# Four transposes per token tile and layer in a two-layer decoder trunk, taken from TensorE to VectorE blocks and DMAs

## The chip, the cores and the metric

The kernel runs on one core of one Trainium2 chip. The metric is the device time of one execution in microseconds (us). The time before is 1190.25 us, the median of three runs (1189.96 to 1190.47). All arithmetic is in float32; products are made from a rounded upper part and a remainder of each operand (type float32r), three matmuls for each product.

## The reference, cut to what matters

The program computes two layers of a decoder trunk over 256 tokens of width 1024. Each layer is a feed-forward part, a mixer and a second feed-forward part, each between two RMS norms. Only the mixer is touched, and in it two things: the short convolution, and the gated sum of the three branches on its way into the output projection.

```python
u, bg, cg, q, kv, nsa_g, q_mem, merge_g = jnp.split(h @ w_in, points, axis=-1)
y_conv = bg * short_conv(cg * u, conv_w)          # conv3 along the tokens, 512 channels
...
g_conv, g_nsa, g_mem = jnp.split(jax.nn.sigmoid(merge_g), 3, axis=-1)
merged = g_conv * (y_conv @ w_br_conv) + g_nsa * (y_nsa @ w_br_nsa) + g_mem * (y_mem @ w_br_mem)
return merged @ w_out
```

## The kernel before, in words

The 256 tokens are two tiles of 128, t = 0 and t = 1. Each tile has a stream of its own through both layers (`stream`, generator functions), and the program is written by a loop that advances one stream by one step at a time. A step is mostly one weight unit: a tile of 128x1024 weights is loaded by SyncE into `raw`, ScalarE rounds it into `whi` (L333), VectorE makes the remainder `wlo` (L334), and TensorE multiplies. Every unit is used by both streams, stream 0 being up to `LEAD` = 3 steps ahead. Splits of units are written `AHEAD` = 4 steps before their use. `later(n, fn)` puts a piece of work n steps on, counted over both streams. Attention, compression and the memory branch run as background tasks between the steps. The order in which each engine finally sees its instructions comes from the framework's scheduler, which works with modelled durations (two of its constants are set at the head of the file); SyncE alone keeps the order written.

A matmul of this kernel has tokens in columns of its left operand, so activations have to be turned from tokens-in-partitions to channels-in-partitions. There are two ways in the kernel before:

- `transpose4` (L441): TensorE multiplies four blocks of 128x128 with an identity into one bank of PSUM, and ScalarE and VectorE read the bank.
- `turn` (L451 to L457): the source is written in an order of columns called lanes (`lanes_out` of the target, `lanes_in` of what is read: every fourth column first), VectorE turns its 32x32 blocks (`nc.vector.transpose`, in the trace STREAM_TRANSPOSE), one step later (`AWAY` = 1) GpSimd issues four DMAs from `blocks` to `moved`, which carry the blocks to their partitions, and after `wait` steps the given function reads `moved`.

In the mixer (`mixer`, L1382 on), stream by stream:

- u is scaled into `us`, then `conv_part` multiplies it with the columns of c into `v`, and `CONV` = 7 steps later transposes `v` with `transpose4`; from the bank come `vT` (with two carried tokens in front) and `cT`, the sum over the three taps.
- `conv_out` scales the columns of the gate into `bs`, `BS` = 4 steps later transposes it, multiplies `cT` with it and splits the product into `yconv`, which the branch product reads after two more column blocks of gates (16 steps over both streams).
- For each branch in `ORDER` and each half n of the 1024 output columns, `gth` times the branch product is summed into `merged0` and `merged1` (L1435 to L1438). After the last branch `transpose_half` transposes half 0 `HALF` = 5 steps later, half 1 at `SECOND` = 2 steps into the output projection, and `evac_split` (L432, L433) splits the bank into `mThi` and `mTlo`.
- `output` multiplies with `w_mix_out` in eight steps k; steps 0 to 3 read half 0, steps 4 to 7 half 1. The last three steps are written bank by bank (`TAIL`).

## Time and profile before

| | |
|---|---|
| median of three runs | 1190.25 us |
| the profiled execution | 1190.01 us |
| its span on the core | 1188.3 us, so 1.7 us lie around it |
| TensorE matmul busy | 1177.2 us, 5777 instructions |
| VectorE busy | 891.7 us |
| ScalarE busy | 755.9 us |
| GpSimd busy | 177.2 us |
| moved by DMA | 260.64 MB |
| granted TensorE clock | 0.999 of full speed |

In the rows of the profile PE is TensorE's matmul queue, PEld its weight load, DVE VectorE, ACT ScalarE, POOL GpSimd, SP SyncE; L441 is line 441 of the kernel before. A group gives its busy time in us and the mean of one instruction in ns, then the idle time of its engine just before it and what ended that. Matmuls overlap, so a matmul's own duration is longer than the distance to the next one.

### The profile page before, as it was taken

To read this page: it belongs to the slowest core of one execution; us is meant where nothing else is said; L and a number is where in the kernel's file an instruction comes from. 1 tells how busy PE (TensorE), PEld (TensorE's weight loads), DVE (VectorE), ACT (ScalarE), POOL (GpSimd) and SP (SyncE) were. 2 spreads that over 40 slices of the span, in tenths; PEclk is the share of its full clock that TensorE was granted. 3 is DMA by queue.
4 is the path that set the end of the run, shared out by engine and by line. 5 is a ranking of instruction groups with operands and counts; after the bars stand their busy time and mean duration, and the time that the engine had idled before them with its cause. 6 is when DMAs were issued, how large, how long until landed. Compare 5 with 4: busy or idle time off the path is not lost.

```text
span 1188.3 us, 16619 instructions
## 1 busy us (share of the span) xinstructions
PE 1177.2 (99%) x5777; PEld 1032.5 (87%) x5777; DVE 891.7 (75%) x1130; ACT 755.9 (64%) x1217; POOL 177.2 (15%) x333
## 2 busy tenths in 40 slices
PE   9999999999999999999999999999999999999997
PEld 7888888888988888888888888889888888888886
DVE  6867757798998786676577677588899977767753
ACT  6655836888885565555465565469889655655541
POOL 4001301411120020011011011014012200110100
PEclk9999999999999999999999999999999999999999
DMA  7787875776678767777767678757767687587771
GB/s 258 253 256 240 276 261 154 228 240 192 194 231 216 247 185 221 222 235 230 228 184 230 215 229 270 240 141 242 232 178 229 198 231 229 178 250 213 234 223 63
DMA packets 133764, 260.64 MB, mean 219 GB/s; under 512 B 15694, under 2 KB 36848, under 8 KB 133680
## 3 DMA queue, kind: packets, MB, share of 16 engines
q1 hardware_dynamic: 124048, 235.11, 63.7%
q0 software_dynamic: 9600, 24.47, 7.6%
q8 instruction: 45, 0.74, 0.3%
q14 instruction: 39, 0.32, 0.1%
q10 hardware_dynamic: 32, 0.01, 0.0%
HBM read 235.42 MB, written 2.10 MB: 200 GB/s over the span
## 4 chain that ended last, share of the span: by engine, by line
PE 95%; ACT 2%; DVE 1%; issue 1%; DMA 0%; POOL 0%; SPq 0%; DVEq 0%; POOLq 0%; ACTq 0%
PE acc L410 35%; PE acc L396 9%; PE acc L397 9%; PE acc L398 9%; PE y L398 7%; PE y L396 7%; PE y L397 7%; PE pt L441 2%; PE br L396 2%; PE br L398 2%; PE br L397 2%; ACT whi L333 1%; PE s L1070 1%; DVE wlo L334 0%; PE om L1268 0%
## 5 line engine op out<-in xcount | busy, mean ns | idle before, releaser
L334 DVE TENSOR_TENSOR wlo<-raw,whi 128x1024 fp32r<-128x1024 f32 (+2 forms) x441 | 529.0, 1211 | 186.0 <-ACT whi L333 182.0
L333 ACT CAST whi<-raw 128x1024 fp32r<-128x1024 f32 (+2 forms) x441 | 452.6, 1040 | 255.2 <-PE acc L410 116.1
L457 POOL DMA_DIRECT2D moved<-blocks x176 | 95.8, 563 | 644.6 <-DVE blocks L451 368.9
L410 PE MATMUL acc<-wlo,hThi 128*128 128x512 f32 x640 | 191.6, 380 | 0.0
L410 PE MATMUL acc<-whi,hTlo 128*128 128x512 f32 x640 | 191.4, 380 | 0.0
L410 PE MATMUL acc<-whi,hThi 128*128 128x512 f32 x640 | 191.4, 381 | 0.0
L396 PE MATMUL acc<-whi,hThi 128*128 128x512 f32 (+1 forms) x480 | 182.8, 381 | 0.0
L397 PE MATMUL acc<-wlo,hThi 128*128 128x512 f32 (+1 forms) x480 | 179.3, 374 | 0.3 <-DVE wlo L334 0.2
L398 PE MATMUL acc<-whi,hTlo 128*128 128x512 f32 (+1 forms) x480 | 178.9, 373 | 0.0
L410 PEld LDWEIGHTS acc<-whi,hTlo 128*128 128x128 f32 x640 | 121.2, 189 | 17.3 <-DVE hTlo L513 0.4
L410 PEld LDWEIGHTS acc<-wlo,hThi 128*128 128x128 f32 x640 | 121.1, 189 | 17.0 <-DVE wlo L334 0.3
L410 PEld LDWEIGHTS acc<-whi,hThi 128*128 128x128 f32 x640 | 120.7, 189 | 16.6
L396 PE MATMUL y<-whi,turnhi 128*128 128x512 f32 x352 | 133.8, 380 | 0.0
L397 PE MATMUL y<-wlo,turnhi 128*128 128x512 f32 x352 | 133.7, 380 | 0.0
L398 PE MATMUL y<-whi,turnlo 128*128 128x512 f32 x352 | 133.7, 380 | 0.0
L398 PEld LDWEIGHTS acc<-whi,hTlo 128*128 128x128 f32 x480 | 90.9, 189 | 11.6
L397 PEld LDWEIGHTS acc<-wlo,hThi 128*128 128x128 f32 x480 | 91.1, 190 | 10.9 <-DVE wlo L334 0.9
L396 PEld LDWEIGHTS acc<-whi,hThi 128*128 128x128 f32 x480 | 91.1, 190 | 10.3
L398 PEld LDWEIGHTS y<-whi,turnlo 128*128 128x128 f32 x352 | 66.7, 189 | 9.2
L397 PEld LDWEIGHTS y<-wlo,turnhi 128*128 128x128 f32 x352 | 66.7, 189 | 9.2
L396 PEld LDWEIGHTS y<-whi,turnhi 128*128 128x128 f32 x352 | 66.7, 189 | 9.2
L475 DVE TENSOR_TENSOR turnlo<-moved,turnhi 128x1024 fp32r<-128x1024 f32 (+1 forms) x42 | 49.1, 1168 | 26.8 <-ACT turnhi L474 26.4
(307 smaller groups left out, 1449.6 us busy)
## 6 DMA issues: line engine op xcount, KB each, us to landing
raw<-in_ffn_w_in_dram SPq DMA_DIRECT2D x159, 512.0 KB, 4.7
raw<-in_w_mix_in_dram SPq DMA_DIRECT2D x96, 512.0 KB, 4.5
raw<-in_ffn_w_out_dram SPq DMA_DIRECT2D x88, 512.0 KB, 4.6
moved<-blocks POOLq DMA_DIRECT2D x144, 128.0 KB, 4.3
raw<-in_ffn_w_in_dram SPq DMA_DIRECT2D x34, 256.0 KB, 4.0
raw<-in_w_mem_kv_dram SPq DMA_DIRECT2D x16, 512.0 KB, 4.6
raw<-in_w_mix_out_dram SPq DMA_DIRECT2D x16, 512.0 KB, 4.9
raw<-in_cmp_k_w_dram SPq DMA_DIRECT2D x8, 512.0 KB, 4.6
```

The source lines that it names most:

```text
L333: pinned(nc.scalar.copy(hi[:, c0:c1], raw[:, c0:c1]))
L334: pinned(nc.vector.tensor_sub(lo[:, c0:c1], raw[:, c0:c1], f32(hi[:, c0:c1])))
L396: nc.tensor.matmul(ps, lhsT=xh, rhs=wh, start=start, stop=False, skip_group_check=skip)
L397: nc.tensor.matmul(ps, lhsT=xh, rhs=wl, start=False, stop=False, skip_group_check=skip)
L398: nc.tensor.matmul(ps, lhsT=xl, rhs=wh, start=False, stop=stop, skip_group_check=skip)
L410: pinned(nc.tensor.matmul(ps[j][:, :n], lhsT=hT[x2][:, k], rhs=moving(w, j * n, n), start=(k == 0 and i == 0), stop=(k == 7 and i == 2)))
L441: pinned(nc.tensor.transpose(pt[:, j * P:(j + 1) * P], src[:, c0 + j * P:c0 + (j + 1) * P], ident))
L457: nc.gpsimd.dma_start(moved[0][:, q * f:(q + 1) * f], blocks[q * 32:(q + 1) * 32, :n].rearrange("j (p f) -> j p f", p=4))
L475: nc.vector.tensor_sub(lv, mv, f32(hv))
L1070: nc.tensor.matmul(s3[:, i], lhsT=QT[:, g * 2 + u, i], rhs=pairs(KT[j][:, var * 2 + g], 0, 256), start=(i == 0 and j == 0), stop=(i == 1 a ...
```

## The change

`v` and `bs` are written in lanes and go through `turn` instead of `transpose4`; the waits `CONV` and `BS` become 9 steps. The sum of a half after the last branch goes into a new tile `laned` in lanes, which goes through `turn` as well, with a wait of 11 steps for half 0 and 8 for half 1 (`MOVED`); what reads `moved` is `place`, and if it hasn't run by then, the output's step 0 (half 0) or step 4 (half 1) runs it. `cT` is now made from `vT` in SBUF, since no bank holds the turned `v`. The factors of the norm are placed so that `v` needs no scale of its own (`r[4]` is the product of two of them).

```diff
+MOVED = {0: 11, 1: 8}
-CONV, BS, CMP, ZC, QS_0, QS_1, QM, PC, YM = 7, 4, 6, 2, 2, 6, 2, 3, 1
+CONV, BS, CMP, ZC, QS_0, QS_1, QM, PC, YM = 9, 9, 6, 2, 2, 6, 2, 3, 1
...
         v = ttile("v")
-        nc.vector.scalar_tensor_tensor(v[:, :512], c_ps, r[0], u_s[:, :512], op0=OP.mult, op1=OP.mult)
+        nc.vector.tensor_tensor(lanes_out(v, 0, [[P, 4]]), lanes_in(u_s, 0, 512), lanes_in(c_ps, 0, 512), op=OP.mult)
         cT = ttile("cT")
-        def turn():
-            pt = transpose4(v, 0)
+        def shifted(mv):
...
-            nc.scalar.copy(vT[:, :, 2:130], pt.rearrange("p (c s) -> p c s", c=4))
+            nc.scalar.copy(view(vT, 2, [[130, 4], [32, 4], [1, 32]]), mv)
...
-                nc.scalar.activation(dst, pt[:, c * P:(c + 1) * P], AF.Copy, scale=w[2])
+                nc.scalar.activation(dst, vT[:, c, 2:130], AF.Copy, scale=w[2])
...
-        later(CONV, turn)
+        turn(v, 512, shifted, CONV)
...
-        nc.scalar.activation(bs[:, :512], b_ps, AF.Copy, scale=r[1])
-        def turn():
-            pt = transpose4(bs, 0)
-            nc.vector.tensor_tensor(cT[:, :512], cT[:, :512], pt, op=OP.mult)
+        nc.scalar.activation(lanes_out(bs, 0, [[P, 4]]), lanes_in(b_ps, 0, 512), AF.Copy, scale=r[0])
+        def gated(mv):
+            nc.vector.tensor_tensor(quarters(cT[:, :512], 4), quarters(cT[:, :512], 4), mv, op=OP.mult)
...
-        later(BS, turn)
+        turn(bs, 512, gated, BS)
...
-        nc.scalar.activation(u_s[:, :512], ps, AF.Copy, scale=r[0])
+        nc.scalar.activation(u_s[:, :512], ps, AF.Copy, scale=r[4])
...
+        def move_half(n, laned, wait):
+            def place(mv):
+                if placed[n]:
+                    return
+                placed[n] = True
+                sl = slice(n * 512, (n + 1) * 512)
+                hv, lv = quarters(mh[:, sl], 4), quarters(ml[:, sl], 4)
+                nc.scalar.copy(hv, mv)
+                nc.vector.tensor_sub(lv, mv, f32(hv))
+            moved = turn(laned, 512, place, wait)
+            return lambda: place(turned_view(moved[0], 512))
...
-                    nc.vector.tensor_add(dst, dst, th[:, :512])
+                    if b == ORDER[2] and n in MOVED:
+                        laned = ttile("laned")
+                        nc.vector.tensor_tensor(lanes_out(laned, 0, [[P, 4]]), lanes_in(merged[n], 0, 512),
+                                                lanes_in(th, 0, 512), op=OP.add)
+                        last_half[n] = move_half(n, laned, MOVED[n])
+                    else:
+                        nc.vector.tensor_add(dst, dst, th[:, :512])
...
         def between(k):
-            if k == SECOND:
+            if k == 0 and 0 in MOVED:
+                last_half[0]()
+            if k == 4 and 1 in MOVED:
+                last_half[1]()
```

Three places show what the scheduler makes of it. The first is VectorE's order in the first layer around the second stream's `v`: `us` and `acc` are its two factors, `pc`, `phc` and `nmm` belong to attention, `cT` is the convolution's sum. Before:

```order
L1284 SCALAR_TENSOR_TENSOR v<-acc,rs,us 128x512
L1207 TENSOR_TENSOR phc<-pt,phc 32x512
L1245 TENSOR_REDUCE nmm<-sm 128x2
L1303 SCALAR_TENSOR_TENSOR cT<-vT,convT,cT 128x128 x2
L1304 SCALAR_TENSOR_TENSOR cT<-vT,convT,cT 128x128 x2
```

Now:

```order
L1285 TENSOR_TENSOR v<-us,acc 128x512
L1246 TENSOR_REDUCE nmm<-sm 128x2
L452 STREAM_TRANSPOSE blocks<-v 128x512
L1208 TENSOR_TENSOR phc<-pt,phc 32x512
L1246 TENSOR_REDUCE nmm<-sm 128x2
L335 TENSOR_TENSOR wlo<-raw,whi 128x1024
L452 STREAM_TRANSPOSE blocks<-bs 128x512
```

The block transposes of `v` and of the first stream's `bs` stand among the splits `wlo`, and the first `cT` has moved four instructions down.

The second place is VectorE's order in the first layer from the sum of half 1 on, stream 0 first (`merged_3092` before, `merged_3086` now), then stream 1. Before:

```order
L433 TENSOR_TENSOR mTlo<-pt,mThi 128x512
L1437 SCALAR_TENSOR_TENSOR gth<-gth,br 128x512
L334 TENSOR_TENSOR wlo<-raw,whi 128x1024
L1438 TENSOR_TENSOR merged_3092<-merged_3092,gth 128x512
L334 TENSOR_TENSOR wlo<-raw,whi 128x1024 x2
L1437 SCALAR_TENSOR_TENSOR gth<-gth,br 128x512
L1438 TENSOR_TENSOR merged_3209<-merged_3209,gth 128x512
L334 TENSOR_TENSOR wlo<-raw,whi 128x1024
L433 TENSOR_TENSOR mTlo<-pt,mThi 128x512
```

Now:

```order
L1452 SCALAR_TENSOR_TENSOR gth<-gth,br 128x512
L1418 TENSOR_TENSOR mTlo<-moved,mThi 128x512
L335 TENSOR_TENSOR wlo<-raw,whi 128x1024
L1455 TENSOR_TENSOR laned<-merged_3086,gth 128x512
L452 STREAM_TRANSPOSE blocks<-laned 128x512
L335 TENSOR_TENSOR wlo<-raw,whi 128x1024 x2
L1452 SCALAR_TENSOR_TENSOR gth<-gth,br 128x512
L335 TENSOR_TENSOR wlo<-raw,whi 128x1024
L1455 TENSOR_TENSOR laned<-merged_3198,gth 128x512
L335 TENSOR_TENSOR wlo<-raw,whi 128x1024
L452 STREAM_TRANSPOSE blocks<-laned 128x512
L1418 TENSOR_TENSOR mTlo<-moved,mThi 128x512
```

Between the product `gth` and the block transpose now stand a remainder of the other stream's half 0 and one split (stream 0), or two splits (stream 1). In the second layer stream 0 has the same company, stream 1 one split.

The third place is TensorE's order in the first layer where stream 1's output comes to half 1 (its step 4; `y0_4252` and `y1_4253` before, `y0_4270` and `y1_4271` now). Before:

```order
L396 MATMUL y0_4194<-whi_4278,mThi_3093 128x512
L397 MATMUL y0_4194<-wlo_4279,mThi_3093 128x512
L398 MATMUL y0_4194<-whi_4278,mTlo_3094 128x512
L396 MATMUL y0_4252<-whi_4231,mThi_3210 128x512
L397 MATMUL y0_4252<-wlo_4232,mThi_3210 128x512
L398 MATMUL y0_4252<-whi_4231,mTlo_3211 128x512
```

Now:

```order
L397 MATMUL y1_4210<-whi_4321,mThi_3087 128x512
L398 MATMUL y1_4210<-wlo_4322,mThi_3087 128x512
L397 MATMUL y0_4270<-whi_4253,mThi_3199 128x512
L398 MATMUL y0_4270<-wlo_4254,mThi_3199 128x512
L397 MATMUL y1_4271<-whi_4253,mThi_3199 128x512
L399 MATMUL y0_4270<-whi_4253,mTlo_3200 128x512
```

Step 4 of stream 1 has gone behind stream 0's last step, and within it the matmuls that read `mThi` come before the first that reads `mTlo`. Counted in TensorE's order of the first layer, 54 matmuls now stand between the last branch matmul of half 1 and the output's step 4 in stream 0 and 59 in stream 1; in the second layer 54 and 52.

More of the change, by code (lines that the diff above doesn't have):

```diff
@@ L1401, in mixer @@
         merged = [ttile(f"merged{n}") for n in range(2)]
+        last_half = [None, None]
         mh, ml = gtile("mThi", F32R), gtile("mTlo", F32R)
@@ L1406, in transpose_half @@
             evac_split(mh[:, sl], ml[:, sl], transpose4(merged[n], 0))
+        placed = [False, False]
+        def move_half(n, laned, wait):
[9 more added lines that the diff above has]
+            return lambda: place(turned_view(moved[0], 512))
         for b in ORDER:
@@ L1437, in mixer @@
                     nc.vector.scalar_tensor_tensor(th[:, :512], th[:, :512], 1.0, pb, op0=OP.add, op1=OP.mult)
-                    nc.vector.tensor_add(dst, dst, th[:, :512])
-                if b == ORDER[2] and n == 0:
+                    if b == ORDER[2] and n in MOVED:
[5 more added lines that the diff above has]
+                        nc.vector.tensor_add(dst, dst, th[:, :512])
+                if b == ORDER[2] and n == 0 and 0 not in MOVED:
                     later(HALF, lambda: transpose_half(0))
@@ L1444, in between @@
         def between(k):
-            if k == SECOND:
+            if k == 0 and 0 in MOVED:
+                last_half[0]()
+            if k == 4 and 1 in MOVED:
+                last_half[1]()
+            if k == SECOND and 1 not in MOVED:
                 transpose_half(1)
```

## The prediction, made before the changed kernel had run

> **What bounds the kernel now.** I read the page first, then TensorE's waits, then the windows of the two mixers, and last single instructions in the timeline. From the page: the span, the engines' busy times, the chain that ended last.
>
> ```profile
> span 1188.3 us, 16619 instructions
> PE 1177.2 (99%) x5777; PEld 1032.5 (87%) x5777; DVE 891.7 (75%) x1130; ACT 755.9 (64%) x1217; POOL 177.2 (15%) x333
> PE 95%; ACT 2%; DVE 1%; issue 1%; DMA 0%; POOL 0%; SPq 0%; DVEq 0%; POOLq 0%; ACTq 0%
> ```
>
> 95% of the chain is TensorE. A busy matmul queue could still be stretched by waits, so the view of its waits is next:
>
> ```profile
> PE pt L441 <- DMA x<-in_x_dram: 1.4, 1, 1.4
> PE idle L205 <- DVE idle L200: 1.1, 1, 1.1
> PE z L1111 <- DVE wlo L334: 1.0, 2, 0.6
> PE pt L441 <- POOL kd L905: 0.4, 1, 0.4
> ```
>
> The four longest kinds of wait make 3.9 us. The kernel's time is therefore the number of matmuls times their spacing, and a matmul taken away is time gained, as long as the others come as early as before. But the mixers, where the change sits, have VectorE close behind:
>
> ```profile
> 280.00:350.00 70.00, 70.00 (x375) 62.27 (x375) 66.90 (x110) 61.19 (x135) 11.34 (x23) 1.00 0.68 207
> 350.00:400.00 50.00, 50.00 (x239) 43.59 (x238) 42.10 (x50) 30.46 (x43) 4.33 (x8) 1.00 0.81 228
> 870.00:950.00 80.00, 80.00 (x421) 70.94 (x420) 77.36 (x117) 67.56 (x148) 16.51 (x31) 1.00 0.66 195
> ```
>
> (Windows; the columns after the length are PE, PEld, DVE, ACT, POOL, then clock, DMA share and GB/s.) VectorE is free for 3.1 us of 70 around the first layer's convolution and 2.6 of 80 around the second's; 7.9 of 50 are free afterwards.
>
> **The change part by part. Removed: 64 transposes.** Groups of TensorE by tile, one group of four in the timeline, and an unbroken stretch of the chain in order of time:
>
> ```profile
> L441 PE MATMUL pt<-ident,merged 128*128 128x128 f32 x32 | 4.8, 273 | 0.0
> L441 PE MATMUL pt<-ident,bs 128*128 128x128 f32 x16 | 2.7, 273 | 0.0
> L441 PE MATMUL pt<-ident,v 128*128 128x128 f32 x16 | 2.4, 273 | 0.0
> 288.54 0.60 PE L441 MATMUL pt<-ident,v 128*128 128x128 f32 x4
> 288.89 0.46 PE L396 MATMUL acc<-whi,hThi 128*128 128x512 f32 x1
> 289.19 0.38 PE L397 MATMUL acc<-wlo,hThi 128*128 128x512 f32 x1
> 289.41 0.38 PE L398 MATMUL acc<-whi,hTlo 128*128 128x512 f32 x1
> ...
> 431.13 95.19 PE acc L410 x441
> ```
>
> 64 instructions are 16 groups of four. An undisturbed 128x512 matmul takes 95.19/441 = 0.216 us. From the start of the group to the second matmul behind it are 0.65 us; less one matmul the group costs 0.434 us (the first matmul behind it is stretched too). 16 x 0.434 = **6.9 us off TensorE**.
>
> The Trainium skill, page TensorE: Matmul & The Clock Gate, section Part 4: PE-mode transpose, has about 275 ns for a transpose in a kernel; the rows' mean of 273 ns agrees. An estimate from that page's figure is 64 x 0.275 = 17.6 us; it prices latency where the queue pays spacing, 0.109 us each here, so I don't use it.
>
> **Added on VectorE.** Rows by form, and one of ScalarE's:
>
> ```profile
> L451 DVE STREAM_TRANSPOSE blocks<-wide 128x1024 f32<-128x1024 f32 x16 | 19.8, 1239 | 0.0
> L451 DVE STREAM_TRANSPOSE blocks<-wide 128x768 f32<-128x768 f32 x8 | 7.8, 975 | 0.1
> L1284 DVE SCALAR_TENSOR_TENSOR v<-acc,rs,us 128x512 f32<-128x512 f32 x4 | 3.0, 746 | 0.0
> L1438 DVE TENSOR_TENSOR merged<-merged,gth 128x512 f32<-128x512 f32 x16 | 10.9, 684 | 0.3
> L1095 DVE TENSOR_TENSOR F<-G,smallT 128x240 f32<-128x240 f32 x8 | 4.2, 572 | 0.1
> L579 DVE TENSOR_TENSOR hTlo<-hf,hThi 128x256 fp32r<-128x256 f32 x20 | 8.1, 420 | 0.6
> L579 DVE TENSOR_TENSOR hTlo<-hf,hThi 128x512 fp32r<-128x512 f32 x10 | 6.9, 685 | 0.0
> L816 ACT COPY mp<-m 128x1024 f32<-128x1024 f32 x2 | 5.9, 2949 | 0.0
> L333 ACT CAST whi<-raw 128x1024 fp32r<-128x1024 f32 x431 | 446.4, 1049 | 255.1 <-PE acc L410 116.1 <-PE y L398 67.5 <-PE acc L398 34.4
> ```
>
> A block transpose of 512 columns is one more step of 256 down the line: 0.975 - 0.264 = 0.71 us. Four for each token tile and layer.
>
> `v` and the two `laned` now read SBUF at every fourth column. No VectorE row does just that. L1095 reads with a wider step: a packed read of 240 would take 0.403 us on the line through L579's rows (0.420 - 16 x 0.00104), it takes 0.572, so 0.70 ns more for an element. ScalarE's L816 reads every fourth column: 2.949 against 1.049 us packed, 1.86 ns more for an element. So a strided 512 on VectorE costs between 0.69 (no penalty) and 1.64 us (ScalarE's); I take 1.05 us (0.685 + 512 x 0.0007), the same engine's row. The Trainium skill, page SBUF — State Buffer, section Door 1: The DMA port swizzle, says that SBUF has lines of 16 bytes, and each access that crosses to a new one pays; a step of four floats does so every time. Rows L816 and L1095 agree, which speaks against the free end.
>
> Per tile and layer: 4 x 0.71 + (1.05 - 0.746) + 2 x (1.05 - 0.684) = 3.9 us, of which `v` and `bs` bring 1.72 (bounds 1.36 and 2.31). Where the weight splits have time this costs nothing. The cushion can be counted: splits made, and matmuls that read `wlo` (four for each split, two from each stream), up to a given time:
>
> ```profile
> 0.00:310.00 310.00, 154.82 (x458) 84.09 (x458) 139.49 (x118) 1.00 0.74 232
> 0.00:945.00 945.00, 481.90 (x1403) 260.68 (x1403) 424.77 (x355) 1.00 0.73 224
> ```
>
> At 310 us 117 splits are made (two of the 118 instructions are halves) and 458/4 = 114.5 used up. Up to three splits wait half used for the stream that is three steps behind, 1.5, so 1.0 is ahead: 12 matmuls, 2.6 us. At 945 us it is 354 - 350.75 - 1.5 = 1.75, so 4.5 us. Against this stand, for two tiles, 3.44 us more VectorE and 4 x 0.434 = 1.74 us by which TensorE comes earlier. Of VectorE's free time I take half as usable, since what ends it is mostly ScalarE's `whi`, which comes no earlier now: 1.5 and 1.3 us. First layer: 3.44 + 1.74 - 1.5 - 2.6 = **1.1 us given back**; second: 3.44 + 1.74 - 1.3 - 4.5, below nothing, so 0. Bounds: 0 (all free time used), and 4.62 + 1.74 - 2.6 = 3.8 plus 4.62 + 1.74 - 4.5 = 1.9, so 5.7. The `laned` sums and their blocks, 4 x (1.05 + 0.71 - 0.684) = 4.3 us a layer, fall behind 350 us into the 7.9 free ones; without that cover they would cost 4.3 us a layer.
>
> **The new wait: half 1 before output step 4.** TensorE, VectorE and a turn in the timeline:
>
> ```profile
> 397.40 0.38 PE L398 MATMUL br<-whi,ynsa 128*128 128x512 f32 x1
> 397.82 0.69 DVE L1437 SCALAR_TENSOR_TENSOR gth<-gth,br 128x512 f32<-128x512 f32 x1
> 398.43 1.22 DVE L334 TENSOR_TENSOR wlo<-raw,whi 128x1024 fp32r<-128x1024 f32 x1
> 360.58 1.24 DVE L451 STREAM_TRANSPOSE blocks<-p 128x1024 f32<-128x1024 f32 x1
> 369.41 1.04 ACT L474 CAST turnhi<-moved 128x1024 fp32r<-128x1024 f32 x1 [2.35 <-DMA moved<-blocks]
> 122.06 0.98 DVE L451 STREAM_TRANSPOSE blocks<-wide 128x768 f32<-128x768 f32 x1
> 129.43 0.84 ACT L474 CAST turnhi<-moved 128x768 fp32r<-128x768 f32 x1 [1.02 <-DMA moved<-blocks]
> L432 ACT CAST mThi<-pt 128x512 fp32r<-128x512 f32 x8 | 4.7, 586 | 6.9 <-PE pt L441 6.9
> L457 POOL DMA_DIRECT2D moved<-blocks x176 | 95.8, 563 | 644.6 <-DVE blocks L451 368.9 <-issue 125.0 <-PE y L398 36.7
> ```
>
> From the end of a block transpose to the reader that waited for the DMAs are 7.59 us (1024 columns) and 6.39 (768); four issues of 0.56 us are in it. For 512 I take 6.39, nearest in size. Budget of stream 0: 54 matmuls x 0.216 = 11.66 us after the last branch matmul ends its turn (397.62). Chain: 0.20 to `gth`, 0.69, the other `mTlo` 0.69, a split 1.22, `laned` 1.05, blocks 0.71, turn 6.39, `mThi` 0.59: 11.54 us, just in time; `mTlo`, 0.69 later, is due two matmuls later (12.09) and 0.14 late. Stream 1 has 59 (12.74 us) and two splits in front: 12.07. Second layer: 11.54 against 11.66, and 10.85 against 52 matmuls, 11.23. Sum about 0.3 us; with 7.59 for the turn the latenesses of `mTlo` are 1.3, 0.6, 1.3 and 1.1, together 4.3. I take **1.0 us**, nearer the smaller transfer. While ScalarE waits in `mThi`, its next `whi` casts stand behind it, and VectorE's `wlo` and later TensorE behind those; the cushion there is filling, as VectorE's 7.9 free us show. Half 0 has 78 matmuls, 16.8 us.
>
> `vT` and `gated` also wait for DMAs, but nine steps (some 1.3 us each) after the blocks against 6.39 to 7.59. On GpSimd 64 more issues are 36 us on 177 of 1188; behind its copy into `carry`, which waits for `vT`, stand `bs`'s four issues, with seven steps in hand. The 4.2 MB more are 1.6% of the bytes. These I price at nothing; if `bs` came ten steps late, `yconv` would block two branch products, 2.6 us.
>
> **Sum**, against the profiled execution of 1190.0 us (span 1188.3, 1.7 around it, 0.24 under the median of the runs): 1190.0 - 6.9 + 1.1 + 1.0 = **1185.2 us**.
>
> **The rivals.** (a) All is hidden: 1190.0 - 6.9 = 1183.1. For it: no wait for `wlo` between 280 and 400 us. Against: VectorE's 95% there. (b) VectorE becomes the bound around the convolutions, strided reads at ScalarE's price: 1190.0 - 6.9 + 5.7 + 1.0 = 1189.8, no difference. For it: L816. Against: L1095. (c) Slower: the halves come late. Place: `mThi` before output step 4. With 7.59 us for each turn and a split more (1.22) in front of each, four halves lose 4.3 + 4.9 = 9.2, and the casts blocked behind ScalarE's wait one split time (1.2) in each of two layers: 1190.0 - 6.9 + 1.1 + 11.6 = 1195.8. It decides from 1.7 us of lateness a half. For it: budgets with a tenth to spare. Against: it needs every turn at its slowest. (d) A transpose held the queue for its whole 273 ns: 1190.0 - 17.5 + 2.1 = 1174.6. Against: the starts at 288.54 and 288.89. That the change doesn't do what it says is excluded by the orders shown: no `v`, `bs` or `merged` is left on TensorE.
>
> **How the numbers follow.** Forecast 0.56, (a) 0.14, (b) 0.17, (c) 0.12, (d) 0.01. A measurement of this kernel tells about 0.2% (2.4 us) from no change. The forecast's own range, both given-back terms from 0.4 to 4.5 together, is 1183.5 to 1187.6, all faster; with (a) and (d), and little of (b), faster is 0.70; same 0.18, from (b) and the near end of (c); slower 0.12. Range 1182.8 to 1191.0: (a), the forecast and (b) whole, (c) mostly left out.
>
> **What would show it.** 5713 matmuls; TensorE's waits in the mixers about 2 us, half for `wlo` between 300 and 350 us, half for `mThi` or `mTlo`; block transposes of 512 at 0.71; `laned` and `v` at 1.05; VectorE about 907 us busy. Waits for `mThi` of over 1.7 us each, or VectorE without a gap through both mixers, would prove it wrong; so would strided sums at 1.6.

## The result and the profile after

The changed kernel takes 1201.37 us (median of four runs, 1200.30 to 1201.50), the kernel before 1190.36 (four runs, 1189.96 to 1190.59). The ratio is 1.0091, with a 95% interval of 1.0073 to 1.0108: 11 us slower, where 5 us faster was forecast, and outside the forecast's range of 1182.8 to 1191.0. (No execution of any run here was in a disturbed state; the ratios and the quotients of the medians differ by some hundredths of a per cent.)

The page of the changed kernel: the span, the busy times, the chain that ended last.

```profile
span 1199.8 us, 16668 instructions
PE 1176.6 (98%) x5713; PEld 1028.3 (86%) x5713; DVE 909.5 (76%) x1146; ACT 756.6 (63%) x1217; POOL 211.0 (18%) x397
PE 58%; DMA 2%; DVE 2%; ACT 2%; issue 1%; POOL 0%; DVEq 0%; POOLq 0%; ACTq 0%
```

TensorE lost its 64 transposes, but its busy time fell by 0.6 us only, because some matmuls took longer. The 58% of the chain that ended last can't be set against the 95% of before: the shares of this line add up to 65% only, since the chain, followed back from the end, breaks off at a transfer `moved<-blocks` at 407 us. Of the part that it covers TensorE still has nine tenths (58 of 65). So it is the waits that show where the kernel is no longer bounded by the number of matmuls. What TensorE waited for, from the view of its waits (us in total, times, longest):

```profile
PE y L397 <- ACT mThi L1417: 8.8, 2, 6.2
PE om L1269 <- ACT yf L1029: 1.9, 1, 1.9
PE s L1041 <- ACT bs L1311: 1.2, 1, 1.2
```

None of the three was there before. The first is the wait for half 1 ahead of output step 4, once in each layer; the other two lie in the convolution parts, at 305 and 892 us. The timeline of TensorE in the second layer shows the longest wait and what comes behind it:

```profile
998.14 0.38 PE L399 MATMUL y<-whi,mTlo 128*128 128x512 f32 x1
1004.69 0.80 PE L397 MATMUL y<-whi,mThi 128*128 128x512 f32 x1 [6.17 <-ACT mThi L1417]
1005.28 0.64 PE L398 MATMUL y<-wlo,mThi 128*128 128x512 f32 x1
...
1009.54 0.45 PE L399 MATMUL y<-whi,mTlo 128*128 128x512 f32 x1
1009.83 0.38 PE L397 MATMUL y<-whi,mThi 128*128 128x512 f32 x1
```

After the wait a matmul takes 0.63 to 0.64 us instead of 0.38, and up to 1009.8 us they start every 0.42 us instead of every 0.216. The windows name the reason (columns after the length: PE, PEld, DVE, ACT, POOL, granted clock, DMA share, GB/s):

```profile
1000.00:1005.00 5.00, 0.31 (x1) 0.31 (x2) 2.83 (x4) 1.64 (x3) 2.18 (x4) 0.79 1.02 366
1005.00:1010.00 5.00, 5.00 (x13) 3.98 (x13) 2.72 (x3) 1.54 (x2) 0.00 (x0) 0.53 0.81 265
```

The granted clock fell to half, so the wait cost about 2.6 us more than its length. And the DMA engines were busy throughout (1.02, 366 GB/s) while the late half's transfers were under way.

The distances between all matmul starts give the place of the loss. From each distance the spacing of an undisturbed matmul is taken off (0.216 us for 512 columns, 0.109 for a transpose or 256 columns), and the rest summed; some records are missing, so a sum is good to a few tenths.

| gaps of TensorE, us | convolution, layer 0 (270 to 330) | late half, layer 0 (392 to 432) | convolution, layer 1 (862 to 912) | late half, layer 1 (975 to 1025) | all four |
|---|---|---|---|---|---|
| before | 2.3 | 1.0 | 1.2 | 1.1 | 5.6 |
| after | 5.8 | 3.8 | 3.6 | 9.5 | 22.7 |

17 us of new gaps, less the 6.9 us that the transposes gave: that is 10 of the 11 us. The work itself, by form (busy us, mean ns, then idle time of the engine just before):

```profile
L1455 DVE TENSOR_TENSOR laned<-merged,gth 128x512 f32<-128x512 f32 x8 | 12.1, 1508 | 0.1
L1285 DVE TENSOR_TENSOR v<-us,acc 128x512 f32<-128x512 f32 x4 | 6.1, 1523 | 0.0
L669 DVE TENSOR_TENSOR wide<-th,acc 128x512 f32<-128x512 f32 x40 | 27.5, 687 | 3.2 <-DVE th L665 0.5
L452 DVE STREAM_TRANSPOSE blocks<-laned 128x512 f32<-128x512 f32 x8 | 5.7, 710 | 0.2
```

A block transpose of 512 costs the forecast 0.71 us. A sum that reads SBUF at every fourth column costs 1.51 us against 0.68 packed, not 1.05. The third row is the surprise: `wide` reads a bank of PSUM at every fourth column (`lanes_in(pb, 0, n)`), and that costs nothing, 0.687 us. The Trainium skill, page SBUF — State Buffer, section Door 1: The DMA port swizzle, speaks of lines of 16 bytes in SBUF and a penalty for each access that crosses to a new one; the trace agrees and sets the price, 1.6 ns an element on VectorE for a step of 16 bytes.

The chain behind the 6.2 us, in the timeline of VectorE, ScalarE and GpSimd:

```profile
981.22 0.71 DVE L452 STREAM_TRANSPOSE blocks<-laned 128x512 f32<-128x512 f32 x1
984.76 2.16 POOL L458 DMA_DIRECT2D moved<-blocks  x4 [4.11 <-DVE wlo L335]
988.82 0.68 DVE L1452 SCALAR_TENSOR_TENSOR gth<-gth,br 128x512 f32<-128x512 f32 x1
991.09 0.62 ACT L1417 CAST mThi<-moved 128x512 fp32r<-128x512 f32 x1 [3.63 <-DMA moved<-blocks]
991.74 0.69 DVE L1418 TENSOR_TENSOR mTlo<-moved,mThi 128x512 fp32r<-128x512 f32 x1 [2.24 <-ACT mThi L1417]
992.35 1.63 DVE L1455 TENSOR_TENSOR laned<-merged,gth 128x512 f32<-128x512 f32 x1
994.99 0.72 DVE L452 STREAM_TRANSPOSE blocks<-laned 128x512 f32<-128x512 f32 x1
1004.02 0.62 ACT L1417 CAST mThi<-moved 128x512 fp32r<-128x512 f32 x1 [3.36 <-DMA moved<-blocks]
```

The first two rows, `mThi` at 991.09 and `mTlo` are stream 1's half 0; the others are stream 0's half 1. Half 0's issue came 2.83 us after its blocks (0.3 to 0.6 for the other turns of the halves). So its reader held ScalarE for 3.63 us and VectorE for 2.24, and behind it in VectorE's queue stood the sum of stream 0's half 1, whose operand had been ready since 989.5. Its own turn then took 8.31 us instead of 6.39. The same steps for stream 0's half 1 in both layers, counted from the end of the last branch matmul's turn, against the 11.65 us (54 matmuls) until output step 4 asks for it:

| us | `gth` starts | `laned` starts after `gth` | turn, blocks to `mThi` | whole chain |
|---|---|---|---|---|
| after, layer 0 | 0.5 | 2.1 | 8.2 | 14.4 |
| after, layer 1 | 2.1 | 2.8 | 8.3 | 17.9 |

### The profile page after: what moved, and what is told of

Read it like the earlier page. It is cut to its first block, busy times and chain, and to the rows that moved or that the text cites. A ratio compares the mean times of both kernels' runs of the same rounds, so it can differ in the third digit from the quotient of the medians.

```text
span 1199.8 us, 16668 instructions
## 1 busy us (share of the span) xinstructions
PE 1176.6 (98%) x5713; PEld 1028.3 (86%) x5713; DVE 909.5 (76%) x1146; ACT 756.6 (63%) x1217; POOL 211.0 (18%) x397
## 4 chain that ended last, share of the span: by engine, by line
PE 58%; DMA 2%; DVE 2%; ACT 2%; issue 1%; POOL 0%; DVEq 0%; POOLq 0%; ACTq 0%
PE acc L411 26%; PE y L397 5%; PE y L399 5%; PE y L398 5%; PE acc L398 4%; PE acc L397 4%; PE acc L399 4%; DMA moved<-blocks 2%; DVE wlo L335 1%; PE pt L442 1%; ACT whi L334 1%; PE br L399 1%; PE br L397 1%; PE br L398 1%; POOL moved L458 0%
## 5 line engine op out<-in xcount | busy, mean ns | idle before, releaser
L458 POOL DMA_DIRECT2D moved<-blocks x240 | 130.4, 564 | 716.4 <-DVE blocks L452 338.7
```

The costliest lines, as they stand in the source:

```text
L458: nc.gpsimd.dma_start(moved[0][:, q * f:(q + 1) * f], blocks[q * 32:(q + 1) * 32, :n].rearrange("j (p f) -> j p f", p=4))
```

## The experiments

After the first comparison there were two theories. One: each part has a price of its own in its own place (by a first count of single gaps, convolution 5.4 us, halves 12.4). Its rival: the parts act on each other.

### Each part alone

```diff
conv_alone
-MOVED = {0: 11, 1: 8}
+MOVED = {}
halves_alone: conv_part, conv_out, CONV, BS and the scale of us as before
```

> Only the convolution's input and gate go by VectorE and DMAs; both halves of the gated sum stay on TensorE (transposes before output step 2, and five steps after the sum). From the gaps of the changed kernel's trace: 32 transposes less are -3.5 us; the gaps in the two convolution parts (2.1 us at 305 and 1.5 of half clock behind it, 1.4 at 892 and 0.4 behind it) are +5.4. Theory 'two costs, each in its own place': 1190.4 - 3.5 + 5.4 = 1192.3 us, with TensorE waiting for the copy of yf near 305 us. Rival 'only the halves hurt, the convolution's gaps follow from them': 1186.9 us and no such wait.

> Only the two halves of the gated sum go by VectorE and DMAs; the convolution's input and gate are back on TensorE with their old delays. Theory 'two costs, each in its own place': 1190.4 - 3.5 (32 transposes) + 12.4 (gaps of 2.8 and 6.3 us before output step 4, 0.7 of smaller ones, 2.6 of half clock behind the longer) = 1199.3 us, waits for mThi of 2.8 and 6.3 us as in the changed kernel. Rival 'VectorE is overloaded by the sum of both parts': each alone fits, 1187 us, waits under 1 us.

Measured: the convolution alone 1192.41 us (ratio 1.0013, 1.0003 to 1.0022), as the first theory had it, though in part by luck: its trace has no half clock behind either wait, and the new gaps in the two convolution parts sum to 3.6 us (last table) instead of 5.4. The halves alone 1191.52 us (1.0007, 0.9998 to 1.0016), 8 us under its 1199.3 and 4.5 over the rival's 1187. The waits of `halves_alone`:

```profile
PE y L397 <- ACT mThi L1419: 1.2, 1, 1.2
PE y L399 <- DVE mTlo L1420: 0.4, 1, 0.4
```

and those of `conv_alone`:

```profile
PE om L1269 <- ACT yf L1029: 1.5, 1, 1.5
PE s L1041 <- ACT bs L1311: 1.2, 1, 1.2
```

So the halves by themselves don't have the long waits; they come when the convolution, 80 us ahead, is moved as well. Alone, the chain of stream 0's half 1 takes 11.6 us in layer 0, near the 11.54 of the prediction, and 13.0 in layer 1. The parts cost 2.0 and 1.2 us by the medians, together 11.0: **7.8 us are an interplay**, for which the prediction had no term.

### One half back on TensorE

```diff
half1_back
-MOVED = {0: 11, 1: 8}
+MOVED = {0: 11}
```

> The convolution and half 0 of the gated sum go by VectorE and DMAs; half 1 is back on TensorE, transposed before output step 2. Theory 'the late half is what hurts': the waits for mThi go, and with them 12.4 us; 16 transposes (1.7 us) come back: 1201.4 - 12.4 + 1.7 = 1190.7 us, 1.7 us under the kernel with the convolution alone. Rival 'half 0 is late too' (its DMAs' reader blocks ScalarE and VectorE): as slow as or slower than the convolution alone, 1193 us or more, with waits for mThi at output step 0.

Measured: 1190.74 us (1.0002, 0.9993 to 1.0012), and no wait for `mThi` in its trace. Against the convolution alone, half 0 gained 1.7 us, the 16 x 0.109 of its transposes; half 1 on top cost 10.6. Half 0 is hidden, as forecast; the interplay is that of the convolution and half 1.

### The strided reads

```diff
packed
-        nc.scalar.activation(u_s[:, :512], ps, AF.Copy, scale=r[4])
+        nc.scalar.activation(lanes_out(u_s, 0, [[P, 4]]), lanes_in(ps, 0, 512), AF.Copy, scale=r[4])
...
-                nc.scalar.activation(ths[n][:, :512], pg, AF.Tanh, scale=r[1])
+                nc.scalar.activation(fours_out(ths[n]), fours_in(pg), AF.Tanh, scale=r[1])
...
-                        nc.vector.tensor_tensor(lanes_out(laned, 0, [[P, 4]]), lanes_in(merged[n], 0, 512),
-                                                lanes_in(th, 0, 512), op=OP.add)
+                        nc.vector.tensor_add(laned[:, :512], dst, th[:, :512])
```

`fours_in` is the step-of-four view over all 512 columns, `fours_out` its packed target; the gated products read their bank of PSUM with `fours_in` too.

> Everything stays moved, but no VectorE sum reads SBUF at every fourth column any more: the reordering is done by the readers of PSUM (us, the gate and the gated products), so v and the two sums read packed. Theory 'the strided read is the root': v and laned fall from 1.51 to 0.69 us, 9.9 us less VectorE; the changed kernel's stalls go as a whole and about 1185 us are left, near the prediction. Rival 'the DMA turn itself is too slow for the late half' (8.2 us from the block transpose to its reader): each late half comes only 0.8 to 1.6 us earlier, waits of 1.5 and 4.5 us stay, 1194 to 1197 us.

Measured: 1197.42 us (1.0057, 1.0041 to 1.0072), 4 us better, just above the rival's 1194 to 1197. The sum is packed and costs 0.686 us, but TensorE still waits (`packed`, by form, and its wait for half 1):

```profile
L1468 DVE TENSOR_TENSOR laned<-merged,gth 128x512 f32<-128x512 f32 x8 | 5.5, 686 | 0.1
```

```profile
PE y L405 <- ACT mThi L1425: 6.9, 2, 4.0
```

In layer 0 the block transpose ended 3.5 us earlier than in the changed kernel (401.45 against 404.91 us; 1.9 of them because the whole stream was ahead), but the turn took 9.9 us instead of 8.2, and the wait was no shorter. Strided reads are a third of the loss, not its root.

### Where the price of the parts lies without strided reads

```diff
halves_packed: halves_alone with the reordering of packed, and the last sum in merged[n] itself
conv_packed: conv_alone with packed's us and v
half0_packed: halves_packed with MOVED = {0: 11}
conv_half0_packed: conv_packed and half0_packed together
```

> Both halves of the gated sum by VectorE and DMAs, convolution on TensorE, the sums kept in the reordered form from PSUM on (no read of SBUF at every fourth column). With the strided sums the chain from the last branch product to mThi took 11.6, 11.4, 13.0 and 12.1 us against budgets of 11.7, 12.7, 11.7 and 11.2. Theory 'the strided read made them late': each chain is 0.8 us shorter, one wait of about 0.5 us is left: 1190.4 - 3.5 + 0.5 = 1187.4 us. Rival 'the turn's DMAs set it, and what VectorE gains is lost in queues': waits of 1 to 2 us as before, 1190 to 1191.5 us.

> The convolution's input and gate alone by VectorE and DMAs, with us kept in the reordered form from PSUM on, so that v reads packed. Theory 'two strided v of 0.83 us each stand ahead of the sum that frees a PSUM bank': the waits for yf and bs fall from 1.5 and 1.2 to 0.7 and 0.4 us and the half clock behind the first goes: 1192.4 - 1.6 - 1.5 = 1189.3 us. Rival 'the added block transposes and the four DMA issues ahead of the memory attention's hold that chain': the waits stay over 1 us, 1192 us.

> Only half 0 of the gated sum goes by VectorE and DMAs, half 1 and the convolution are on TensorE as before; half 0's sums are kept in the reordered form from PSUM on, so that no sum reads SBUF at every fourth column, and the last sum goes into the tile of the gated sum itself (one temporary less). Theory 'a turn costs nothing where 78 matmuls stand between': 16 transposes less, 16 x 0.109 = 1.74 us: 1190.4 - 1.7 = 1188.6 us, no wait for mThi. Rival 'its DMAs and VectorE's blocks disturb the weights anyway': 1190 us or more.

> The convolution's input and gate and half 0 by VectorE and DMAs, half 1 on TensorE, no strided read of SBUF anywhere. Theory 'half 0 is hidden also on a thin cushion': 1190.0 (convolution alone, packed) - 1.7 = 1188.3 us. Rival 'on a thin cushion half 0's reader holds VectorE and ScalarE': 1190 us or more.

| | us, median | ratio | interval | expected |
|---|---|---|---|---|
| halves_packed | 1188.61 | 0.9984 | 0.9975 to 0.9993 | 1187.4 |
| conv_packed | 1189.99 | 0.9997 | 0.9988 to 1.0006 | 1189.3 |
| half0_packed | 1188.88 | 0.9988 | 0.9979 to 0.9997 | 1188.6 |
| conv_half0_packed | 1188.31 | 0.9985 | 0.9975 to 0.9994 | 1188.3 |

Packed reads are worth 2.9 us for the halves, 2.4 for the convolution, and three of these kernels are faster than the kernel before, by 0.12 to 0.16%. In `halves_packed` the wait for half 1 has all but gone (0.2 us).

The convolution breaks even: it still gives back the 3.5 us of its transposes. Of its waits, that for `yf` is 1.1 us instead of 1.5 and that for `bs` 0.3 instead of 1.2, so the first theory on them was right for the second only; the half clock that it wanted to remove isn't in the trace of `conv_alone`. What makes the other (the block transposes, the taps that now stand in one piece, or `v`'s four DMA issues ahead of the memory attention's) was not separated.

### The interplay: only one layer

```diff
conv_layer0
-        cT = conv_part(t, l, u_s, ps, r)
+        cT = (conv_part if l == 0 else conv_part_pe)(t, l, u_s, ps, r)
```

(`conv_part_pe` and `conv_out_pe` are those of the kernel before.)

> As the changed kernel, but in the second layer the convolution's input and gate are back on TensorE; both halves of the gated sum stay moved in both layers. Theory 'the convolution eats the cushion of split weights, and the late half of the same layer pays': in the second layer the wait for mThi falls from 6.2 to 1.2 us (as with the halves alone), the 2.6 us of half clock behind it and the convolution's 1.8 us of gaps go, 16 transposes (1.7 us) come back: 1201.4 - 5.0 - 2.6 - 1.8 + 1.7 = 1193.7 us; the first layer's wait of 2.8 us stays. Rival 'the late half is slow by itself' (strided sums, DMAs, whatever the convolution does): the wait of 6.2 us stays, 1201 us.

Measured: 1194.98 us (1.0034, 1.0021 to 1.0047). Stream 0's chain in layer 1 takes 13.05 us, as with the halves alone (13.00), and 14.3 in layer 0, as in the changed kernel (14.4). TensorE waits for `mThi` three times now, 4.5 us together, the longest 2.5 us in layer 0 and 1.3 in layer 1 (1.2 were expected there). So what the convolution does to the late half, it does within its own layer. But this run alone can't tell by what, since it also moved GpSimd's late issue (below) out of the mixer.

### The half clock

```diff
filled
                 last_half[1]()
+                if t == 0 and l == 1:
+                    fill = tbank()
+                    for _ in range(24):
+                        tc.keep_in_program_order(nc.tensor.matmul(fill, lhsT=mh[:, :P], rhs=mh[:, :512],
+                                                                  start=True, stop=True))
```

> The changed kernel with 24 more matmuls (5.2 us, into a bank that nobody reads) ahead of output step 4 of stream 0 in the second layer, where TensorE waited 6.2 us. Theory 'the wait itself lowers the clock': the matmuls behind it go at 0.216 us instead of 0.43, the granted clock stays at 1.0 there, and 2.6 us come back: 1198.8 us. Rival 'the slow matmuls have another reason' (weights, operands that come late): 0.43 us each stays, 1201 us.

Measured: 1198.18 us (1.0065, 1.0051 to 1.0079), 3.2 us less with 24 matmuls more. TensorE and the clock behind the filled wait, from its timeline and its windows:

```profile
999.86 5.62 PE L1473 MATMUL pt<-mThi 128*128 128x512 f32 x24
1006.22 0.48 PE L397 MATMUL y<-whi,mThi 128*128 128x512 f32 x1 [0.75 <-ACT mThi L1417]
1007.27 0.38 PE L397 MATMUL y<-whi,mThi 128*128 128x512 f32 x1
1007.48 0.38 PE L398 MATMUL y<-wlo,mThi 128*128 128x512 f32 x1
```

```profile
1005.00:1010.00 5.00, 4.23 (x19) 3.05 (x18) 3.05 (x3) 2.62 (x3) 0.90 (x2) 1.00 0.98 331
```

The half came as late as before, but the matmuls behind it keep their spacing at a granted clock of 1.00. The wait itself had lowered the clock.

### The weight loads

```diff
held
         raw = rawp.tile([P, 1024], F32, name="raw")
+        if parts[0][2] == "ffn2_w_in" and held.get(parts[0][3], 0) and touched.setdefault(parts[0][3], 0) < 3:
+            touched[parts[0][3]] += 1
+            nc.scalar.copy(raw[:, 0:1], f32(held[parts[0][3]][:, 512:513]))
```

(The first three loads of the second feed-forward network overwrite a column that ScalarE has written from `mThi`, so they wait for it; they are also written only once it is.)

> The changed kernel, but the first weight loads of the second feed-forward network wait in each layer until stream 0's half 1 has been read (mThi). Theory 'the late half's DMAs share the DMA engines with the weight loads': from the block transpose to mThi it takes 6.3 instead of 8.2 and 8.3 us, the two waits fall from 2.8 and 6.2 to about 0.9 and 4.2 us: 1197.5 us. Rival 'only queues on VectorE and ScalarE make it late': 8.2 us and both waits stay, 1201 us or, with the loads late, more.

Measured: 1198.38 us (1.0067, 1.0054 to 1.0081), 3.0 us less. In layer 1 the turn takes 6.03 us instead of 8.31, in layer 0 7.58 instead of 8.17. The two waits:

```profile
PE y L403 <- ACT mThi L1423: 5.9, 2, 3.8
```

So the weight loads do slow the turn, by 2.3 us in layer 1 and 0.6 in layer 0. Busy DMA engines alone don't tell when: with the halves alone their share is 0.90 and 0.98 from 400 to 410 us, while the turn of layer 0 takes 6.2 us. What remains in layer 1 is the chain ahead of the turn: `laned` still starts 2.8 us after `gth`.

### GpSimd's late issue

In every trace the 123rd DMA that GpSimd issues starts 3.1 to 3.5 us after its block transpose, and in every kernel of the record so far that has as many, the 227th starts 2.8 to 3.2 us after it, with GpSimd idle just before. (Issues with other work of GpSimd right ahead of them are late as well, by 1.6 to 3.6 us in the moved convolution.) In the kernel before the 123rd fell on a feed-forward turn (692.8 us), where nobody waited. With 32 issues more in each layer, the 227th is the first of stream 1's half 0 in layer 1 (984.76 us).

```diff
shifted
+    apart = dram.tile([P, 72 * 16], F32, name="apart", tag="apart", bufs=1)
+
+    def small(i):
+        for j in range(i, i + 4):
+            tc.keep_in_program_order(nc.gpsimd.dma_start(apart[:, j * 16:(j + 1) * 16], ident[:, 0:16]))
+
+    if not dry:
+        for i in range(0, 72, 4):
+            later(432 + i // 6, lambda i=i: small(i))
shifted_held: both edits
```

> The changed kernel with 72 more small DMAs issued by GpSimd (128 x 16 floats each, into a scrap of DRAM) between 560 and 640 us, where GpSimd has nothing to do; the orders of the other engines are the same. In all traces so far GpSimd's 123rd DMA, and where there are as many its 227th, starts 2.8 to 3.4 us after its block transpose instead of 0.3 to 0.6, whatever it carries; in the changed kernel the 227th is the first of stream 1's half 0 in the second layer. Theory 'the count decides': that DMA now starts 0.3 to 0.6 us after its blocks, nothing blocks VectorE ahead of stream 0's late sum, the second wait for mThi falls from 6.2 to about 3 us, as in the first layer, and the half clock behind it (2.6 us) goes: 1201.4 - 3.3 - 2.6 = 1195.5 us. Rival 'the place decides' (what VectorE does there): 2.8 us late again, 1201 us.

> The small DMAs of the run before and, with them, the weight loads held back until stream 0's half 1 has been read. Theory 'late issue, shared DMA engines and thin cushion add up': both waits for mThi fall to 1 to 2.4 us and no half clock is left behind them: 1198.4 (loads held alone) - 3.3 - 1.5 = 1193.6 us. Rival 'one of the two is enough': not below the run with the small DMAs alone.

Measured: `shifted` 1200.50 us (1.0086, 1.0072 to 1.0099), `shifted_held` 1197.85 (1.0064, 1.0050 to 1.0078). The issue went where the theory had it (timeline of `shifted`, VectorE and GpSimd; 0.29 us after the blocks):

```profile
981.65 0.71 DVE L452 STREAM_TRANSPOSE blocks<-laned 128x512 f32<-128x512 f32 x1
982.65 2.16 POOL L458 DMA_DIRECT2D moved<-blocks  x4 [1.53 <-DVE blocks L452]
```

but the time hardly moved. (The small DMAs run from 613 to 655 us in this trace, not to 640, and hold back two feed-forward turns there; TensorE has 0.3 us of gaps between 613 and 720 us.) `laned` in layer 1 now starts 0.5 us after `gth` instead of 2.8; yet `gth` itself starts 2.7 us late instead of 2.1, the wait is 4.0 us, and the half clock is still there in part. The theory on the issue was right, that on its price wrong: 1 us instead of 6, which isn't clear of the scatter (kernels with four executions each can be told apart from about 2.5 us on). VectorE was behind with or without it. `shifted_held` has no half clock behind its waits, as expected, and its longest wait for `mThi` is 2.4 us, but it missed its 1193.6 by 4 us and is no faster than `held` beyond the scatter.

### The cushion of split weights

SyncE loads weights as soon as a buffer of raw weights is free, that is when its split is done. The row in which its queue reaches `gB` comes right behind the last load of the output weights. In `halves_alone`:

```profile
400.04 0.59 SPq L292 DMA_DIRECT2D gB<-in_mix_norm_post_dram  x1
984.55 0.59 SPq L292 DMA_DIRECT2D gB<-in_mix_norm_post_dram  x1
```

and in the changed kernel:

```profile
406.63 0.59 SPq L292 DMA_DIRECT2D gB<-in_mix_norm_post_dram  x1
995.72 0.59 SPq L292 DMA_DIRECT2D gB<-in_mix_norm_post_dram  x1
```

Against the end of stream 0's last branch matmul (397.4 and 983.2 us with the halves alone, 399.3 and 986.7 in the changed kernel) the last of these loads has been issued 2.6 and 1.3 us later in the one, 7.4 and 9.0 in the other. The cushion (splits made less a quarter of the matmuls that read `wlo`, as in the prediction, but without its deductions for half and half-used splits, which are much the same in all kernels; windows of `halves_alone`, then of the changed kernel):

```profile
0.00:380.00 380.00, 189.93 (x551) 101.59 (x552) 169.18 (x143) 1.00 0.74 231
0.00:980.00 980.00, 500.29 (x1453) 269.58 (x1454) 441.13 (x369) 1.00 0.73 225
```

```profile
0.00:380.00 380.00, 189.33 (x548) 101.74 (x549) 166.04 (x140) 1.00 0.75 230
0.00:980.00 980.00, 499.18 (x1448) 269.60 (x1448) 437.87 (x366) 1.00 0.74 225
```

143 - 551/4 = 5.25 and 369 - 1453/4 = 5.75 splits with the halves alone, 3.0 and 4.0 in the changed kernel. The convolution takes about two splits off the cushion, and VectorE doesn't win them back before the output. Two runs test whether that is the cause: one gives VectorE time back in the changed kernel, the other adds time to the halves alone, without a DMA and close behind the convolution: its doubled subtractions start between 319 and 333 us and between 910 and 925. The moved convolution itself adds 4 x (1.52 - 0.75) + 8 x 0.71 = 8.8 us of VectorE, some 30 us earlier in each layer.

```diff
relieved
-        lo = wp.tile([P, 1024], F32R, name="wlo")
+        lo = hi if item[3][0][2] == "w_branch_conv" else wp.tile([P, 1024], F32R, name="wlo")
...
+            if item[3][0][2] != "w_branch_conv":
                 pinned(nc.vector.tensor_sub(lo[:, c0:c1], raw[:, c0:c1], f32(hi[:, c0:c1])))
burdened (in halves_alone)
+            for _ in range(2 if item[3][0][2] == "w_branch_conv" else 1):
                 pinned(nc.vector.tensor_sub(lo[:, c0:c1], raw[:, c0:c1], f32(hi[:, c0:c1])))
relieved_shifted: relieved with shifted's small DMAs
```

> The changed kernel without the low part of the convolution branch's weights: its four units in each layer have no wlo (TensorE reads whi in its place, as many matmuls), so VectorE has 4 x 1.22 = 4.9 us less to do in each layer, between the convolution and the late halves; the result leaves that part out. Theory 'VectorE's added time comes out of the cushion of split weights, and without it everything at the late halves runs late': the cushion at 380 and 980 us is back at 5 splits or more instead of 3 and 4, both waits for mThi fall to 1 to 2 us, and only the two separate costs are left: 1190.4 + 2.0 + 1.2 = 1193.6 us. Rival 'the turns are late because of the DMAs and GpSimd': waits of 2.8 and 6 us stay, 1200 us.

> The mirror of the run before: the halves alone (convolution on TensorE), with the subtraction for wlo done twice for the convolution branch's four units in each layer: 4.9 us more VectorE per layer at the place where the moved convolution had its own, no DMA more. Theory of the cushion: the waits for mThi of 1.2 and 0.4 us grow to 2.5 to 4 us each, 1195 to 1197 us. Rival 'the turns are late because of the DMAs and GpSimd': as with the halves alone, 1191.5 to 1192.5 us.

> The changed kernel with VectorE relieved (no wlo for the convolution branch's weights, which the result leaves out) and with the 72 small DMAs that keep GpSimd's 227th issue away from the late halves. Theory 'thin cushion and late issue add up': of the relieved kernel's waits of 1.8 and 2.5 us the second falls to about 1, the slower matmuls behind it go: 1197.6 - 2.5 = 1195 us. Rival 'the late issue costs nothing beyond what the thin cushion already costs': 1197.5 us, the second wait stays at 2.5.

Measured: `burdened` 1198.52 us (1.0066, 1.0049 to 1.0083), **7.0 us over the halves alone, by 9.8 us of VectorE with no DMA more** (3.5 to 5.5 were expected). Its waits, its two `gB` rows, and its splits:

```profile
PE y L398 <- ACT mThi L1420: 5.9, 2, 3.5
```

```profile
404.55 0.59 SPq L292 DMA_DIRECT2D gB<-in_mix_norm_post_dram  x1
996.84 0.60 SPq L292 DMA_DIRECT2D gB<-in_mix_norm_post_dram  x1
```

```profile
0.00:380.00 380.00, 189.99 (x552) 101.70 (x552) 171.06 (x145) 1.00 0.74 229
0.00:980.00 980.00, 497.83 (x1444) 268.48 (x1444) 444.99 (x373) 1.00 0.73 222
```

Without the four and eight doubled subtractions its cushion is 145 - 4 - 552/4 = 3.0 and 373 - 8 - 1444/4 = 4.0 splits, just that of the changed kernel.

The convolution's blocks and DMAs aren't needed for the late half to be late. But the scheduler orders VectorE and ScalarE anew for each of these kernels: between stream 0's `gth` and its `laned` in layer 0 stands one split in `halves_alone`, and in `burdened`, as in the changed kernel, the other stream's `mTlo` as well, so that `laned` starts 1.97 us after `gth` instead of 1.05. So what is shown as the cause is VectorE's added work together with the order that the scheduler makes of it; what the time alone costs was not separated, and the order of `relieved` differs from that of the changed kernel too. With less cushion alone the last of the loads is issued 7.4 us after the last branch matmul in both layers, the turns take 7.9 and 9.1 us instead of 6.2 and 6.8, and the busy DMA engines of the changed kernel come back in its window:

```profile
1000.00:1005.00 5.00, 1.46 (x8) 0.95 (x7) 2.46 (x4) 0.82 (x2) 2.16 (x4) 1.00 1.00 366
```

`relieved`: 1197.61 us (1.0066, 1.0051 to 1.0081), 4 us better than the changed kernel, where 8 were expected (its cushion is 139 - 535/4 = 5.25 splits at 380 us and 359 - 1418/4 = 4.5 at 980, where 5 or more were); `relieved_shifted`: 1195.19 us (1.0047, 1.0029 to 1.0065), as expected. The waits for half 1 in `relieved`, and its splits:

```profile
PE y L398 <- ACT mThi L1418: 4.2, 2, 2.5
0.00:380.00 380.00, 183.72 (x535) 98.47 (x535) 163.59 (x139) 1.00 0.75 232
0.00:980.00 980.00, 486.85 (x1418) 262.92 (x1418) 429.30 (x359) 1.00 0.73 226
```

and in `relieved_shifted`:

```profile
PE y L398 <- ACT mThi L1427: 2.7, 3, 2.0
```

By the medians the late issue was worth 0.9 us on the thin cushion and 2.4 on the better one. Neither is clear of the scatter, so that the two hide each other isn't shown; with both taken away the time comes within 1.7 us of the sum of the separate prices (1193.5). The gaps by place, all kernels of this part:

| gaps, us | convolution, layer 0 | late half, layer 0 | convolution, layer 1 | late half, layer 1 |
|---|---|---|---|---|
| halves_alone | 2.3 | 2.5 | 1.2 | 2.6 |
| conv_alone | 4.3 | 1.0 | 2.8 | 1.7 |
| after | 5.8 | 3.8 | 3.6 | 9.5 |
| shifted | 4.4 | 5.4 | 3.4 | 6.7 |
| held | 4.5 | 3.4 | 3.4 | 7.4 |
| shifted_held | 4.5 | 3.6 | 3.1 | 5.7 |
| relieved | 4.4 | 3.2 | 4.3 | 6.1 |
| relieved_shifted | 4.4 | 4.7 | 4.1 | 2.9 |
| burdened | 2.5 | 8.5 | 2.3 | 6.3 |

(A row is one execution, not the median: that of `burdened` is 2.6 us slower than its median, that of `conv_alone` 1.0 faster.) In layer 1 the late half's gaps come down to those of the halves alone (2.9 against 2.6) once VectorE is relieved and the late issue moved. In layer 0 no edit of the changed kernel takes them under 3 us, and `burdened` has 8.5 there, more than the changed kernel; what holds them beside the cushion stays open.

## Why the prediction was wrong, point by point

- **Removed, 6.9 us: right.** 5713 matmuls; half 0's 16 transposes gave 1.7 us on the chip, twice (`half1_back` against `conv_alone`, `conv_half0_packed` against `conv_packed`), which is 16 x 0.109. Rival (d), 273 ns each, is out.
- **Added on VectorE: the size of one row was wrong.** Blocks 0.71 as forecast. The strided sums cost 1.51 us, near the upper bound of 1.64 from ScalarE's row and not at the 1.05 of the same engine's: 12 x 0.46 = 5.5 us more VectorE, 909.5 busy instead of 907 (other rows fell). The row chosen had a different step and 240 elements; the one with the same step was the right neighbour.
- **The convolution, 1.1 us given back: near the upper bound of 5.7.** 5.5 us (1192.41 is 2.0 over before, plus 3.5 of transposes), of which 2.4 are the strided `v`. And not as a wait for `wlo`, as forecast, but for `yf` and `bs`, which hold banks of PSUM: work that ScalarE and VectorE do later, in a queue that was priced only for its splits.
- **Half 1, 1.0 us: wrong, the step that failed.** Alone, the halves gave back 4.6 us (1.2 + 3.5), just over the upper bound of 4.3, with a chain of 11.6 us in layer 0 as worked out and 13.0 in layer 1. With the convolution moved it was 14.4 and 17.9. Against the 11.54 of the forecast, in layer 0 the turn is 1.8 us too long and the strided sum 0.6, and 0.5 is queue; in layer 1 it is 1.9, 0.6 and 3.9, the last all work of VectorE ahead of `gth`, of `laned` and of its blocks. The prediction took the chain's durations from a trace in which the cushion is whole, and added the two parts' costs as if they were independent. It said that the cushion is spent at 310 us, and that VectorE has 7.9 us free behind 350, and did not join the two: with a thin cushion every sum and every reader of `moved` stands behind splits that can't wait, and the weight loads come later and meet the late half's DMAs. Busy shares didn't tell of it: VectorE is busy for 66.9 of 70 us and 77.3 of 80 in the windows of the convolutions, as before, and from 350 to 400 us it still had 5.3 us free instead of 7.9.
- **Half 0, GpSimd and DMA bytes priced at nothing:** half 0 right. For GpSimd, the 36 us of issues are indeed hidden, but the place of its late issue was overlooked (0.9 to 2.4 us, not clear of the scatter). For DMA, 4.2 MB are no load, but four transfers of 64 KB among six loads of 512 KB were 2.3 us late in layer 1.
- **Rival (c), slower: the right mechanism, too cheap and too unlikely.** Place (`mThi` ahead of output step 4) and sign are as it said, and the point of 1.7 us a half was passed. It gave 1195.8 and the chance of 0.12; it lacked the half clock (2.6 us), the waits of the convolution and the interplay.
- **What would show it:** waits of over 1.7 us for `mThi` and strided sums at 1.6 were named as what proves it wrong, and both came (1.51 for the sums). VectorE without a gap through both mixers, the third sign, did not.

## What to carry to other kernels

Where an engine's stock of work done ahead is part of the budget, two edits that draw on it must be priced in sequence: the second one meets the engine without its stock, with its queue later and the weight loads at another time. A reordering read of SBUF costs VectorE more than twice a packed one here, and the same read of PSUM nothing: do it where the data leaves PSUM. A turn through DMAs pays where the reader is far away (half 0, 78 matmuls: 1.7 us gained in each of two pairs of runs), and is a risk of several us where its budget has a tenth of a microsecond to spare.

## What the runs showed of the hardware that was not expected

- **GpSimd's issue that comes late by count.** The 123rd and the 227th DMA of GpSimd came 2.8 to 3.5 us after their blocks in all kernels that have so many and no small DMAs, whatever they carry and wherever they stand (the 227th between 983 and 1146 us). With 72 small DMAs after the 123rd, GpSimd paused for 2.4 us ahead of the 229th and the 333rd instead, again 104 apart. The cause isn't shown; what can be planned is where it falls.
- **A wait of two microseconds can halve the clock.** A gap of 6.2 us gave half clock until 5 us after its end, a gap of 2.1 us at 303 us gave half clock from 306.6 to 310.0, and one of 2.8 us at 411 us none, while in `conv_layer0` a wait of 2.5 us at that place did (the third row):

```profile
305.00:310.00 5.00, 4.67 (x20) 4.00 (x21) 4.87 (x12) 4.68 (x9) 4.16 (x8) 0.66 0.79 220
410.00:415.00 5.00, 2.32 (x10) 1.39 (x9) 3.11 (x5) 1.93 (x3) 2.16 (x4) 1.00 0.98 350
410.00:415.00 5.00, 2.92 (x7) 2.29 (x8) 3.41 (x5) 3.29 (x4) 2.16 (x4) 0.72 1.02 375
```

The Trainium skill, page TensorE: Matmul & The Clock Gate, section Part 1: The HAM clock gate, has a window of about 3.4 us that runs free and lowers the clock after an idle one. The trace agrees with the length (3.4 us of half clock at 306.6) and with the free running (the longer gap did nothing), but the 3.4 us ahead of 306.6 held some ten matmuls, so a window needn't be idle throughout.
- **Price of a stride by memory.** At every fourth column of four bytes VectorE takes 0.69 us for 512 elements out of PSUM and 1.51 out of SBUF.
